# Stationary weights with a step of two, at eight places in turn

## The chip, the cores and the metric

The kernel runs on one core of one Trainium2 chip. The core has a matmul engine (PE; its weight loads are listed apart as PEld), a vector engine (DVE), a scalar engine (ACT), GpSimd (POOL) and a queue engine (SP) that issues the transfers. A matmul has two operands in the core's memory: a stationary one of 128 x 128 that is loaded into the array first, and a moving one whose columns are streamed through it; the result is added up in one of eight banks (128 x 512 words). The metric is the device time of one execution in microseconds. A profile of one execution gives the times of single instructions.

## What is computed

One layer of a decoder: 256 rows of 2048 channels, all float32. A combined input projection, two kinds of attention, an output projection, and a gated MLP with a causal convolution of width 3; each half is normalised and added to its input. Cut to its matrix products:

```python
h = rmsnorm(x, pre_mix_g[l])
proj = h @ w_in[l]                       # 2048 x 5392: q, k, v of two groups, forget gates
...
mix = jnp.concatenate([o_a, o_b], axis=-1) @ w_out[l]
x = x + rmsnorm(mix, post_mix_g[l])
h = rmsnorm(x, pre_ffn_g[l])
u = causal_dwconv(h @ w_up[l], conv_w[l], conv_b[l])      # 2048 x 11264
gate, val = jnp.split(u, 2, axis=-1)
y = (jax.nn.gelu(gate, approximate=True) * val) @ w_down[l]   # 5632 x 2048
x = x + rmsnorm(y, post_ffn_g[l])
```

## The kernel before

Every product of float32 numbers is made of three products of a shorter float format: each operand is split into a high part (rounded) and a low part (what is left), and high x high, high x low and low x high are added up. The weights pass through the core once. They come in units of 128 partitions x up to 1024 words (512 KB), by SP's queue, into five buffers `raw`. ACT makes the high part `whi` with a cast (L111, or L94 in `w_high`), DVE the low part `wlo` with a subtraction raw - whi (L114, or L97). There are five buffers of each part. The order on PE is that of the program; in some stretches the orders of ACT, DVE, POOL and SP are written out too.

Weights are used in two ways.

*Stationary weights* (`still=True`). In the input projection of queries and keys and in the whole up-projection the result is wanted with channels on the partitions. A unit holds 4 blocks of 128 rows of w (index `a`) and 256 channels, those of bank m = 0 and then those of bank m = 1, in each block. For each `a` and `m`, 128 x 128 weights are loaded, and the transposed activations `hT` stream past: 512 columns for a high part of the weights (256 of the activations' high part and 256 of their low part, L252), and 256 columns for a low part of the weights (L257). `proj_T` takes two units at a time: 14 matmuls of high parts, 16 of low parts, and the last 2 of high parts, the two banks by turns. With the pair before, runs of 16 and 16 arise. The very first projections go through `unit_T` (L220 high, L225 low), the first gate of the MLP through `first_gate` (L881 high, L877 low).

*Moving weights.* In the value projection, the output projection and the down projection (`mm3`, L275) the activations are stationary, and the weights are streamed.

Before the change a stationary block is read word after word: 128 words, 512 bytes. The high part lies at the start of its tile of 1024 words, the low part of stationary weights 80 words into its tile of 1152 words (`LOW`), the low part of moving weights at the start. `hT` and the high parts begin at multiples of 512 bytes.

After a projection ACT and DVE add a bank's two halves (L846, L847), POOL scales, and ACT and DVE do the convolution (L850 to L854), the gate (L918, L925) and the split of the result into G.

Of the kernel before, what the change touches and what calls it, by code (L numbers as in the profile page):

```python
# [8 lines left out]
F32 = mybir.dt.float32  # L9
F32R = mybir.dt.float32r  # L10
BF16 = mybir.dt.bfloat16
AF = mybir.ActivationFunctionType
ALU = mybir.AluOpType
# [4 lines left out]
P = 128  # L18
# [4 lines left out]
KT = D // P  # L23
# [7 lines left out]
def hybrid_layer(ctx: ExitStack, tc: tile.TileContext, x, pre_mix_g, w_in, b_forget, sinks,  # L31
# [3 lines left out]
    pe, act, dve, pool, sp = nc.tensor, nc.scalar, nc.vector, nc.gpsimd, nc.sync  # L35
# [6 lines left out]
    wp = ctx.enter_context(tc.tile_pool(name="wp", bufs=4))  # L42
# [20 lines left out]
    UNIT = 1024  # L63
    WB = 5
# [6 lines left out]
        return raw, a, c  # L71


    LOW = 80

    def w_parts(n, keep=None, still=False):


        if keep and keep[0] is None:
            return keep[1]  # L80
        if keep:
            return [keep[0].tile([P, UNIT], F32R, tag="h" + x, bufs=keep[1], name="w" + x)[:, :n]
                    for x in ("hi", "lo")]
        hi = wp.tile([P, UNIT], F32R, tag="whi", bufs=WB, name="whi")
        lo = wp.tile([P, UNIT + 128], F32R, tag="wlo", bufs=WB, name="wlo")
        c = LOW if still else 0
        return [hi[:, :n], lo[:, c:c + n]]

    def w_high(unit, keep=None, still=False):

        raw, a, c = unit
        n = a * c
        hi, lo = w_parts(n, keep, still)
        act.copy(hi, raw[:, :n])  # L94

        def low():
            dve.tensor_tensor(lo, raw[:, :n], hi.bitcast(F32), op=ALU.subtract)  # L97

        return [x.rearrange("p (a c) -> p a c", a=a) for x in (hi, lo)], low

    def w_split(unit, pin=False, keep=None, begun=None, between=None, still=False):

        raw, a, c = unit
        n = a * c
        hi, lo = begun or w_parts(n, keep, still)
        for i in range(2 if between else 1):
            cs = slice(i * 512, i * 512 + 512) if between else slice(0, n)
            if i:
                between()
            if not between or i:  # L110
                i1 = act.copy(hi[:, cs], raw[:, cs])  # L111
                if pin:
                    tc.keep_in_program_order(i1)
            i2 = dve.tensor_tensor(lo[:, cs], raw[:, cs], hi[:, cs].bitcast(F32), op=ALU.subtract)  # L114
            if pin:
                tc.keep_in_program_order(i2)
        return [x.rearrange("p (a c) -> p a c", a=a) for x in (hi, lo)]

    def w_unit(src, a, c, keep=None):
        return w_split(w_load(src, a, c), keep=keep)  # L120
# [21 lines left out]
    first = [[], []]  # L142
    head = wp.tile([P, UNIT], F32, tag="raw", bufs=5, name="raw")
    for i in range(2):
        cs = slice(i * 256, (i + 1) * 256)
# [39 lines left out]
    hT = main.tile([P, KT, 512], F32R, tag="hT", name="hT")  # L185
# [27 lines left out]
    def unit_T(parts, u, banks, ticks=True, halves=False):  # L213

        hi, lo = parts

        def high(a):
            kt = u * 4 + a
            for m, b in enumerate(banks):
                pe.matmul(b, hi[:, a, m * P:(m + 1) * P], hT[:, kt, :], start=(kt == 0),  # L220
                          stop=(kt == KT - 1))

        def low(a):
            for m, b in enumerate(banks):
                pe.matmul(b[:, 256:512], lo[:, a, m * P:(m + 1) * P],  # L225
                          hT[:, u * 4 + a, 0:256], start=False, stop=False)

        high(0)
        high(1)
        if halves:  # L230
            low(0)
            low(1)
        high(2)
        if ticks:
            tick()
        for a in range(2 if halves else 0, 4):
            low(a)
        high(3)
        if ticks:
            tick()  # L240

    def proj_T(w, c0, banks):

        for v in (0, 2):
            parts = [w_split(w_load(w_rows(w, u * 4, 4, c0, 256), 4, 256), still=True)
                     for u in (v, v + 1)]
            steps = [(u, a) for u in range(2) for a in range(4)]

            def high(u, a):
                kt = (v + u) * 4 + a  # L250
                for m, b in enumerate(banks):
                    pe.matmul(b, parts[u][0][:, a, m * P:(m + 1) * P], hT[:, kt, :],  # L252
                              start=(kt == 0), stop=(kt == KT - 1))

            def low(u, a):
                for m, b in enumerate(banks):
                    pe.matmul(b[:, 256:512], parts[u][1][:, a, m * P:(m + 1) * P],  # L257
                              hT[:, (v + u) * 4 + a, 0:256], start=False, stop=False)

            for n, (u, a) in enumerate(steps[:-1]):  # L260
                high(u, a)
                if n in (2, 5):
                    tick()
            for n, (u, a) in enumerate(steps):
                low(u, a)
                if n == 4:
                    tick()
            high(*steps[-1])
            tick()
# [11 lines left out]
    with tc.tile_pool(name="mixp", bufs=1) as mp:  # L281
# [47 lines left out]


        begun = w_parts(UNIT, still=True)
        tc.keep_in_program_order(dve.tensor_copy(begun[0][:, 0:512], head[:, 0:512]))
        x_part(0, (0,), "acc")
        bkv = [bank("att"), bank("att")]
        bq0 = [bank(), bank()]
        for u in range(4):
            if u:
                parts = w_split(first[0][u], True, still=True)
            else:
                parts = w_split(first[0][u], True, begun=begun,  # L340
                                between=lambda: x_part(0, (1,), "acc"))
            if u < 2:
                first_load(u + 2)
            unit_T(parts, u, bkv, False, u == 0)
            if u:
                x_square((2, 3, 2)[u - 1])
            parts = w_split(first[1][u], True, still=True)
            if u == 0:
                x_square(1)
            if u < 3:  # L350
                x_part(u + 1, (0, 1))
            else:
                for t in range(2):
                    st = small.tile([P, 1], F32, tag="st", name="st")
                    dve.tensor_reduce(st, sqx[t], axis=AX.X, op=ALU.add)
                    rpre.append(rstd_of(st, D, f"rpre{t}"))
                    dpre.append(diag_of(rpre[t]))
                later(2, rows_pre)
            unit_T(parts, u, bq0)
# [237 lines left out]
        for p0, npair, cols in ((0, 3, 384), (3, 3, 384), (6, 2, 272)):  # L597
# [3 lines left out]
            for k0 in range(0, KT, per):  # L601
                na = min(per, KT - k0)
                hi, lo = w_unit(w_rows(w_in, k0, na, c0, cols), na, cols)
                for a in range(na):
                    kt = k0 + a
# [104 lines left out]
        hT = hT2  # L710
# [55 lines left out]
        for n in (2, 3):  # L766
            for u in range(4):
                raw = w_load(w_rows(w_out, 8 + u * 2, 2, n * 512, 512), 2, 512)
# [43 lines left out]
    with tc.tile_pool(name="ffn", bufs=1) as fp:  # L812
# [45 lines left out]
        def first_gate():  # L858

            banks = [bank(), bank()]  # L860

            def one(t, u):
                ts = slice(t * P, t * P + P)

                both = u >= 2
                ls = slice(0, 256) if both else ts

                def v(x):
                    return x.rearrange("p (h t c) -> p h t c", h=2, t=2)[:, :, t, :]

                for low in (False, True)[:1 if both and t == 0 else 2]:
                    for kt in range(u * 4, u * 4 + 4):
                        hi, lo = gate[kt]
                        for m, b in enumerate(banks):
                            ms = slice(m * P, (m + 1) * P)
                            if low:
                                pe.matmul(b[:, 256 + ls.start:256 + ls.stop], lo[:, ms],  # L877
                                          hT[:, kt, ls], start=False,
                                          stop=(t == 1 and kt == KT - 1))
                            else:  # L880
                                pe.matmul(v(b), hi[:, ms], v(hT[:, kt, :]),  # L881
                                          start=(t == 0 and kt == 0), stop=False)

            one(0, 0)
            one(0, 1)
            one(0, 2)
            for high, low in [turn(1, u) for u in range(4)]:
                high()
                low()
            one(0, 3)  # L890
            lows[2]()
            x_squares(0)
            x_squares(1)
            rows = ffn_tables()
            for u in range(4):
                one(1, u)
            later(4, rows)
            return banks
# [3 lines left out]
        for half in range(2):  # L902
# [42 lines left out]
            for n in range(3 + (half == 0)):  # L945
                b2 = [bank(), bank()]
                for u in range(FHALF // 2):
                    hi, lo = w_unit(w_rows(w_down, half * FHALF + u * 2, 2, n * 512, 512), 2, 512)
# [33 lines left out]
        for u in range(FHALF // 2):  # L982
            hi, lo = w_unit(w_rows(w_down, FHALF + u * 2, 2, 1536, 512), 2, 512,
                            keep=(None, [rest[:, c:c + 2, :].rearrange("p a c -> p (a c)")
                                         for c in (4 * (u - LAST), 4 * (u - LAST) + 2)])
# [57 lines left out]
```

## Time and profile before

| | |
|---|---|
| median of 2 runs | 1080.03 us (1079.7 to 1080.36) |
| the profiled execution | 1079.4 us, span 1077.6 us |
| PE busy in the span | 1064.9 us, 99% |
| weight loads, busy | 926.9 us, 86% |
| DVE, ACT, POOL busy | 743.8, 619.4, 180.5 us |
| transferred | 202.88 MB, 188 GB/s in the mean |

The stretches of stationary weights lie at the start, in the attention part and in the up-projection (two halves); the moving weights' long stretches follow each half of the up-projection. Matmuls are pipelined, and their ends in the trace are modelled: a matmul's length there is longer than the time from its start to the next one's. The pace is therefore read from starts. The granted clock of PE is full nearly everywhere.

```profile
PE   9999999999999999999999999999999999999996
PEld 7899988887889888888888888888888888888886
DVE  5988878887568876777677444457777777765563
PEclk9999999999999999999999999999999999999999
```

Each digit is the busy share, in tenths, of a fortieth of the span.

### The profile page before, as it was taken

What the parts mean: (1) busy time and instruction counts of PE and PEld (TensorE: products, weight loads), DVE (VectorE), ACT (ScalarE), POOL (GpSimd) and SP (SyncE); (2) the same over time, 40 slices, a digit from 0 to 9 for tenths busy, and PEclk for the clock granted to TensorE, in tenths of its full rate; (3) what the DMA queues carried; (4) which work ended last, traced back from release to release, by engine and by line L of the source; (5) the groups of instructions that cost most, each with busy time, mean ns of one, the idle gap of its engine ahead of it and who ended that gap; (6) DMA issues with size and microseconds to landing.
All of it is one profiled execution on the core that took longest, in us unless ns stands there. A gap on an engine that the chain in (4) does not pass through costs nothing.

```text
span 1077.6 us, 16247 instructions
## 1 busy us (share of the span) xinstructions
PE 1064.9 (99%) x5986; PEld 926.9 (86%) x5986; DVE 743.8 (69%) x1200; ACT 619.4 (57%) x1060; POOL 180.5 (17%) x252
## 2 busy tenths in 40 slices
PE   9999999999999999999999999999999999999996
PEld 7899988887889888888888888888888888888886
DVE  5988878887568876777677444457777777765563
ACT  7766766667557755656565443456565555644450
POOL 3343244332022201101010000001010100101111
PEclk9999999999999999999999999999999999999999
DMA  8645556544863765555665666665556656565652
GB/s 294 209 120 172 176 171 207 159 149 156 300 227 112 235 193 192 194 189 186 194 193 180 200 197 191 195 192 190 186 192 193 193 182 195 188 198 193 193 166 78
DMA packets 164970, 202.88 MB, mean 188 GB/s; under 512 B 6780, under 2 KB 130972, under 8 KB 164380
## 3 DMA queue, kind: packets, MB, share of 16 engines
q1 hardware_dynamic: 164176, 201.27, 58.3%
q8 instruction: 47, 0.77, 0.3%
q10 hardware_dynamic: 716, 0.58, 0.2%
q14 instruction: 31, 0.25, 0.1%
HBM read 199.58 MB, written 2.11 MB: 187 GB/s over the span
## 4 chain that ended last, share of the span: by engine, by line
PE 89%; DVE 4%; ACT 2%; POOL 2%; issue 2%; DMA 2%; SPq 0%; POOLq 0%; DVEq 0%; ACTq 0%
PE bank_acc L275 34%; PE bank_acc L252 19%; PE bank_att L252 14%; PE bank_acc L257 10%; PE bank_att L257 7%; DVE wlo L114 2%; POOL scr L408 1%; PE bank_att L441 1%; PE bank_acc L881 1%; ACT p L459 1%; PE bank_att L476 1%; DMA x_in<-in_x_dram 1%; PE bank_acc L877 0%; ACT whi L111 0%; DMA c_dram<-scr 0%
## 5 line engine op out<-in xcount | busy, mean ns | idle before, releaser
L114 DVE TENSOR_TENSOR wlo<-raw,whi 128x1024 fp32r<-128x1024 f32 (+3 forms) x357 | 454.2, 1275 | 246.8 <-ACT whi L111 173.6
L111 ACT CAST whi<-raw 128x1024 fp32r<-128x1024 f32 (+3 forms) x356 | 367.9, 1035 | 182.2 <-PE bank_acc L275 117.4
L252 PE MATMUL bank_acc<-hT,whi 128*128 128x512 f32 x1088 | 266.9, 392 | 0.0
L252 PEld LDWEIGHTS bank_acc<-hT,whi 128*128 128x128 f32 x1088 | 198.2, 188 | 37.3
L275 PE MATMUL bank_acc<-whi,G 128*128 128x512 f32 (+1 forms) x724 | 214.5, 378 | 0.0
L275 PEld LDWEIGHTS bank_acc<-whi,G 128*128 128x128 f32 x724 | 133.8, 188 | 25.6
L252 PE MATMUL bank_att<-hT,whi 128*128 128x512 f32 x640 | 154.2, 391 | 0.0
L848 POOL TENSOR_TENSOR u<-u,rowf 128x256 f32<-128x256 f32 x88 | 55.5, 653 | 538.3 <-DVE u L847 536.0
L257 PEld LDWEIGHTS bank_acc<-hT,wlo 128*128 128x128 f32 x1088 | 138.3, 189 | 5.7
L257 PE MATMUL bank_acc<-hT,wlo 128*128 128x256 f32 x1088 | 141.8, 281 | 0.0
L252 PEld LDWEIGHTS bank_att<-hT,whi 128*128 128x128 f32 x640 | 117.6, 188 | 22.7
L275 PE MATMUL bank_acc<-wlo,G 128*128 128x512 f32 (+1 forms) x362 | 137.1, 379 | 0.0
L257 PEld LDWEIGHTS bank_att<-hT,wlo 128*128 128x128 f32 x640 | 81.0, 189 | 3.1
L275 PE MATMUL bank_acc<-whi,oT 128*128 128x512 f32 (+1 forms) x272 | 82.5, 380 | 0.0
L257 PE MATMUL bank_att<-hT,wlo 128*128 128x256 f32 x640 | 82.0, 281 | 0.0
L275 PEld LDWEIGHTS bank_acc<-wlo,G 128*128 128x128 f32 x362 | 68.1, 188 | 12.7
L275 PEld LDWEIGHTS bank_acc<-whi,oT 128*128 128x128 f32 x272 | 50.2, 188 | 9.3
L275 PE MATMUL bank_acc<-wlo,oT 128*128 128x512 f32 (+1 forms) x136 | 51.2, 377 | 0.0
L275 PE MATMUL bank_acc<-whi,hT 128*128 128x384 f32 (+1 forms) x192 | 47.5, 323 | 0.0
L846 ACT COPY cs<-bank_acc 128x256 f32<-128x256 f32 x48 | 15.9, 372 | 52.2 <-PE bank_acc L252 52.2
L459 ACT ACTIVATE p<-p,nm 128x256 f32<-128x256 f32 (+1 forms) x64 | 28.4, 445 | 26.9 <-DVE nm L447 26.9
L846 ACT COPY cs<-bank_att 128x256 f32<-128x256 f32 x40 | 13.3, 373 | 47.2 <-PE bank_att L252 47.2
(200 smaller groups left out, 1016.4 us busy)
## 6 DMA issues: line engine op xcount, KB each, us to landing
raw<-in_w_up_dram SPq DMA_DIRECT2D x176, 512.0 KB, 3.5
raw<-in_w_down_dram SPq DMA_DIRECT2D x88, 512.0 KB, 4.6
raw<-in_w_in_dram SPq DMA_DIRECT2D x51, 512.0 KB, 4.1
raw<-in_w_out_dram SPq DMA_DIRECT2D x32, 512.0 KB, 4.7
raw<-in_w_in_dram SPq DMA_DIRECT2D x16, 384.0 KB, 3.4
cb<-c_dram SPq DMA_DIRECT2D x8, 256.0 KB, 3.6
x_sb<-in_x_dram SPq DMA_DIRECT2D x2, 1024.0 KB
raw<-in_w_in_dram SPq DMA_DIRECT2D x5, 408.0 KB, 3.2
```

The costliest lines, as they stand in the source:

```text
L111: i1 = act.copy(hi[:, cs], raw[:, cs])
L114: i2 = dve.tensor_tensor(lo[:, cs], raw[:, cs], hi[:, cs].bitcast(F32), op=ALU.subtract)
L252: pe.matmul(b, parts[u][0][:, a, m * P:(m + 1) * P], hT[:, kt, :], start=(kt == 0), stop=(kt == KT - 1))
L257: pe.matmul(b[:, 256:512], parts[u][1][:, a, m * P:(m + 1) * P], hT[:, (v + u) * 4 + a, 0:256], start=False, stop=False)
L275: pe.matmul(b, a, r[:, cols], start=(first and i == 0), stop=(last and i == 2))
L408: pool.tensor_tensor(dst, dst, row, op=ALU.mult)
L441: pe.matmul(sb[e][:, cs], a[r, t * P:(t + 1) * P], b[r, 0:nk], start=(n == 0), stop=(n == 2))
L459: act.activation(p[:, e, cs], p[:, e, cs], AF.Exp, bias=nm[:, t, e:e + 1], scale=-1.0, accum_out=rs[:, t, e:e + 1])
L476: pe.transpose(pb[:, i * P:(i + 1) * P], p[:, e, c:c + P], ident)
L846: act.copy(c, b[:, 256:512])
L848: pool.tensor_tensor(u[:, 2:258], u[:, 2:258], rowf, op=ALU.mult)
L881: pe.matmul(v(b), hi[:, ms], v(hT[:, kt, :]), start=(t == 0 and kt == 0), stop=False)
```

## The change

In a tile of stationary weights the channels of the two banks now alternate word by word: the block of `a` holds channel 0 of bank 0, channel 0 of bank 1, channel 1 of bank 0, and so on. `w_views` gives the three views that the cast and the subtraction use: `raw` is read in the order in which it came, `hi` and `lo` are written (and `hi` read again) with a step of two words. A matmul takes `hi[:, a, m]`: 128 words with a step of two, out of 1024 bytes. The moving operand, the products and their order stay as they were.

The place of a part in its tile is no longer 0 for the high and 80 words for the low. It goes round eight places, 8 words (32 bytes) apart; two units that follow each other share a place; the low part goes round in another order than the high part, so that in time all pairs of places occur. Both tiles have 1088 words now (1024 and 1152 before), so the buffers of both parts, moving weights included, lie at another distance from each other. All else in memory stays where it was.

```diff
-    LOW = 80
+    still_no = [0]
...
-        hi = wp.tile([P, UNIT], F32R, tag="whi", bufs=WB, name="whi")
-        lo = wp.tile([P, UNIT + 128], F32R, tag="wlo", bufs=WB, name="wlo")
-        c = LOW if still else 0
-        return [hi[:, :n], lo[:, c:c + n]]
+        i = still_no[0] // 2
+        still_no[0] += still
+        cs = (i % 8 * 8, (i // 8 * 3 + i) % 8 * 8) if still else (0, 0)
+        return [wp.tile([P, UNIT + 64], F32R, tag="w" + x, bufs=WB, name="w" + x)[:, c:c + n]
+                for x, c in zip(("hi", "lo"), cs)]
+
+    def w_views(raw, hi, lo, a, still):
+
+        if still:
+            return (raw.rearrange("p (a m i) -> p a m i", a=a, m=2),
+                    *(x.rearrange("p (a i m) -> p a m i", a=a, m=2) for x in (hi, lo)))
+        return [x.rearrange("p (a c) -> p a c", a=a) for x in (raw, hi, lo)]
...
-        act.copy(hi, raw[:, :n])
+        raw, hi, lo = w_views(raw[:, :a * c], *w_parts(a * c, keep, still), a, still)
+        act.copy(hi, raw)
...
-                    pe.matmul(b, parts[u][0][:, a, m * P:(m + 1) * P], hT[:, kt, :],
-                              start=(kt == 0), stop=(kt == KT - 1))
+                    pe.matmul(b, parts[u][0][:, a, m], hT[:, kt, :], start=(kt == 0),
+                              stop=(kt == KT - 1))
...
-                    pe.matmul(b[:, 256:512], parts[u][1][:, a, m * P:(m + 1) * P],
+                    pe.matmul(b[:, 256:512], parts[u][1][:, a, m],
                               hT[:, (v + u) * 4 + a, 0:256], start=False, stop=False)
```

`w_split`, `unit_T` and `first_gate` are changed in the same way.

More of the change, by code (lines that the diff above doesn't have):

```diff
@@ L83, in w_parts @@
                     for x in ("hi", "lo")]
-        hi = wp.tile([P, UNIT], F32R, tag="whi", bufs=WB, name="whi")
-        lo = wp.tile([P, UNIT + 128], F32R, tag="wlo", bufs=WB, name="wlo")
-        c = LOW if still else 0
-        return [hi[:, :n], lo[:, c:c + n]]
+        i = still_no[0] // 2
[8 more added lines that the diff above has]
+        return [x.rearrange("p (a c) -> p a c", a=a) for x in (raw, hi, lo)]
     def w_high(unit, keep=None, still=False):
         raw, a, c = unit
-        n = a * c
-        hi, lo = w_parts(n, keep, still)
-        act.copy(hi, raw[:, :n])
+        raw, hi, lo = w_views(raw[:, :a * c], *w_parts(a * c, keep, still), a, still)
+        act.copy(hi, raw)
         def low():
-            dve.tensor_tensor(lo, raw[:, :n], hi.bitcast(F32), op=ALU.subtract)
-        return [x.rearrange("p (a c) -> p a c", a=a) for x in (hi, lo)], low
+            dve.tensor_tensor(lo, raw, hi.bitcast(F32), op=ALU.subtract)
+        return [hi, lo], low
     def w_split(unit, pin=False, keep=None, begun=None, between=None, still=False):
         raw, a, c = unit
-        n = a * c
-        hi, lo = begun or w_parts(n, keep, still)
+        raw, hi, lo = w_views(raw[:, :a * c], *(begun or w_parts(a * c, keep, still)), a, still)
         for i in range(2 if between else 1):
-            cs = slice(i * 512, i * 512 + 512) if between else slice(0, n)
+            r = slice(i * 2, i * 2 + 2) if between else slice(0, a)
             if i:
@@ L110, in w_split @@
             if not between or i:
-                i1 = act.copy(hi[:, cs], raw[:, cs])
+                i1 = act.copy(hi[:, r], raw[:, r])
                 if pin:
                     tc.keep_in_program_order(i1)
-            i2 = dve.tensor_tensor(lo[:, cs], raw[:, cs], hi[:, cs].bitcast(F32), op=ALU.subtract)
+            i2 = dve.tensor_tensor(lo[:, r], raw[:, r], hi[:, r].bitcast(F32), op=ALU.subtract)
             if pin:
                 tc.keep_in_program_order(i2)
-        return [x.rearrange("p (a c) -> p a c", a=a) for x in (hi, lo)]
+        return [hi, lo]
     def w_unit(src, a, c, keep=None):
@@ L219, in high @@
             for m, b in enumerate(banks):
-                pe.matmul(b, hi[:, a, m * P:(m + 1) * P], hT[:, kt, :], start=(kt == 0),
-                          stop=(kt == KT - 1))
+                pe.matmul(b, hi[:, a, m], hT[:, kt, :], start=(kt == 0), stop=(kt == KT - 1))
         def low(a):
             for m, b in enumerate(banks):
-                pe.matmul(b[:, 256:512], lo[:, a, m * P:(m + 1) * P],
-                          hT[:, u * 4 + a, 0:256], start=False, stop=False)
+                pe.matmul(b[:, 256:512], lo[:, a, m], hT[:, u * 4 + a, 0:256], start=False,
+                          stop=False)
         high(0)
@@ L331, in hybrid_layer @@
         begun = w_parts(UNIT, still=True)
-        tc.keep_in_program_order(dve.tensor_copy(begun[0][:, 0:512], head[:, 0:512]))
+        raw0, hi0, _ = w_views(head, *begun, 4, True)
+        tc.keep_in_program_order(dve.tensor_copy(hi0[:, 0:2], raw0[:, 0:2]))
         x_part(0, (0,), "acc")
@@ L339, in hybrid_layer @@
             else:
-                parts = w_split(first[0][u], True, begun=begun,
+                parts = w_split(first[0][u], True, still=True, begun=begun,
                                 between=lambda: x_part(0, (1,), "acc"))
@@ L874, in one @@
                         for m, b in enumerate(banks):
-                            ms = slice(m * P, (m + 1) * P)
                             if low:
-                                pe.matmul(b[:, 256 + ls.start:256 + ls.stop], lo[:, ms],
+                                pe.matmul(b[:, 256 + ls.start:256 + ls.stop], lo[:, m],
                                           hT[:, kt, ls], start=False,
@@ L880, in one @@
                             else:
-                                pe.matmul(v(b), hi[:, ms], v(hT[:, kt, :]),
+                                pe.matmul(v(b), hi[:, m], v(hT[:, kt, :]),
                                           start=(t == 0 and kt == 0), stop=False)
```

## The prediction

> **What bounds the kernel now.** I read the page first: the span, the busy row of the matmul engine and the chain that ended last.
>
> ```profile
> span 1077.6 us, 16247 instructions
> PE 1064.9 (99%) x5986; PEld 926.9 (86%) x5986; DVE 743.8 (69%) x1200; ACT 619.4 (57%) x1060; POOL 180.5 (17%) x252
> PE 89%; DVE 4%; ACT 2%; POOL 2%; issue 2%; DMA 2%; SPq 0%; POOLq 0%; DVEq 0%; ACTq 0%
> PE bank_acc L275 34%; PE bank_acc L252 19%; PE bank_att L252 14%; PE bank_acc L257 10%; PE bank_att L257 7%; DVE wlo L114 2%; POOL scr L408 1%; PE bank_att L441 1%; PE bank_acc L881 1%; ACT p L459 1%; PE bank_att L476 1%; DMA x_in<-in_x_dram 1%; PE bank_acc L877 0%; ACT whi L111 0%; DMA c_dram<-scr 0%
> ```
>
> The matmul queue never rests, and half of the chain (19 + 14 + 10 + 7 = 50%) lies in the lines that the change touches, L252 and L257. A busy PE can still be a waiting PE, so the waits come next. These are all that PE has:
>
> ```profile
> PE bank_acc L168 <- DVE junk L163: 1.3, 1, 1.3
> PE bank_att L441 <- ACT keys L278: 0.9, 1, 0.9
> PE bank_att L441 <- DVE keys L279: 0.8, 1, 0.8
> PE bank_acc L300 <- DMA x_in<-in_x_dram: 0.6, 1, 0.6
> PE bank_att L300 <- DMA x_in<-in_x_dram: 0.2, 1, 0.2
> ```
>
> 3.8 us in all, none of it in L252 or L257. So nothing feeds PE too late; what counts is the pace at which one matmul follows another. That pace is read from the timeline of the up-projection (start, length, line, count): from the start of one run to the start of the next, divided by the count.
>
> ```profile
> 504.83 2.05 PE L257 MATMUL bank_att<-hT,wlo 128*128 128x256 f32 x16
> 506.72 3.81 PE L252 MATMUL bank_att<-hT,whi 128*128 128x512 f32 x16
> 510.37 2.05 PE L257 MATMUL bank_att<-hT,wlo 128*128 128x256 f32 x16
> ```
>
> A high part (512 columns): (510.37 - 506.72)/16 = 228.1 ns. A low part (256 columns): (506.72 - 504.83)/16 = 118.1 ns. What would they cost if they only streamed columns? Two places with stationary operands at round addresses give it, the down projection and the first gate:
>
> ```profile
> 600.17 0.62 PE L275 MATMUL bank_acc<-whi,G 128*128 128x512 f32 x2
> 600.62 0.39 PE L275 MATMUL bank_acc<-wlo,G 128*128 128x512 f32 x1
> 600.85 0.62 PE L275 MATMUL bank_acc<-whi,G 128*128 128x512 f32 x2
> ...
> 336.40 1.12 PE L881 MATMUL bank_acc<-hT,whi 128*128 128x256 f32 x8
> 337.36 1.00 PE L877 MATMUL bank_acc<-hT,wlo 128*128 128x128 f32 x8
> ...
> 341.05 1.91 PE L728 MATMUL bank_att<-ident,x_sb 128*128 128x128 f32 x16
> ...
> L728 PE MATMUL bank_att<-ident,x_sb 128*128 128x128 f32 x32 | 4.0, 272 | 0.0
> ```
>
> 512 columns: 0.68/3 = 226.7 ns; 256 columns: 0.96/8 = 120.0 ns. The difference is 106.7 ns for 256 columns, 0.417 ns a column, and 120.0 - 106.7 = **13.3 ns of every matmul are not columns**. The transposes (L728) stream 128 columns, 53 ns, and still need (1.91 - 0.27)/15 = 109.3 ns each: there the load of 128 weights is what takes the time. 109.3 ns are 262 column times, which fits two for each weight and 6 (2.5 ns) for the change of weights. So of the 13.3 ns some 2.5 look unavoidable, and 10.8 look like two readers in each other's way: while a matmul streams, the next weights are read beside it. One thing in the rows says that addresses matter: L257's low parts lie 80 words into their tile, and go at 118.1 ns where L881's, as wide and at place 0, go at 120.0.
>
> [...]
>
> **The change, part by part.** No instruction is added, removed or moved: the same casts, subtractions, loads and matmuls in the same order, with other addresses.
>
> 1. *Stationary reads with a step of two.* These groups get them:
>
> ```profile
> L252 PE MATMUL bank_acc<-hT,whi 128*128 128x512 f32 x1088 | 266.9, 392 | 0.0
> L252 PE MATMUL bank_att<-hT,whi 128*128 128x512 f32 x640 | 154.2, 391 | 0.0
> L257 PE MATMUL bank_acc<-hT,wlo 128*128 128x256 f32 x1088 | 141.8, 281 | 0.0
> L257 PE MATMUL bank_att<-hT,wlo 128*128 128x256 f32 x640 | 82.0, 281 | 0.0
> L220 PE MATMUL bank_att<-hT,whi 128*128 128x512 f32 x32 | 9.0, 398 | 0.1
> L225 PE MATMUL bank_att<-hT,wlo 128*128 128x256 f32 x32 | 4.7, 284 | 0.0
> L881 PE MATMUL bank_acc<-hT,whi 128*128 128x256 f32 x64 | 9.1, 287 | 0.0
> ```
>
> 1728 highs and 1728 lows (108 times 3.65 + 1.89 us = 598 us), 64 and 64 in the first projections (each row again for the other banks), 64 and 48 in the first gate. Today the two readers walk at different speeds: a weight takes two column times, so the weights advance 4 bytes while the moving columns advance 8. The faster walks past the slower again and again, and meets it wherever the two need the same part of the memory. With a step of two the weights also advance 8 bytes in two column times. Two readers at equal speed either never meet, or meet once, one waits, and they are apart from then on. I take this reading, since it is the one by which a place can count at all. Bounds: the gain can't exceed what leaves the streams alone. High: 228.1 - (213.3 + 2.5) = 12.3 ns, times 1728 = 21.3 us. Low: 118.1 - 109.3 (the load's own time) = 8.8 ns, times 1728 = 15.2 us. The 240 others: about 2 us. Together 38.5 us. I take nine tenths, 34.7 us, because some of the eight places must start with a meeting.
>
> 2. *Strided writes by ACT and DVE, strided reads by DVE.* These are the rows of a stretch of up-projection, with the busy shares of that stretch (PE, PEld, DVE, ACT, POOL, clock, DMA share, GB/s):
>
> ```profile
> L114 DVE TENSOR_TENSOR wlo<-raw,whi 128x1024 fp32r<-128x1024 f32 x36 | 47.2, 1312 | 24.4 <-ACT whi L111 9.1 <-issue 6.1 <-PE bank_acc L257 5.5
> L111 ACT CAST whi<-raw 128x1024 fp32r<-128x1024 f32 x37 | 38.8, 1048 | 10.0 <-PE bank_acc L252 5.8 <-PE bank_att L252 4.2
> 400.00:500.00 100.00, 100.00 (x581) 88.38 (x579) 72.94 (x107) 59.24 (x91) 11.18 (x18) 1.00 0.59 190
> ```
>
> I cost them at nothing. The cover is DVE's idle 27.1 us of 100: 36 subtractions may grow by 0.75 us each, from 1.31 to 2.06, before DVE and not PE sets the pace. No row of this trace has an ACT or DVE operand with a step, so from below it is nothing and from above a doubling (rival 2). [...]
>
> 3. *Other places for the moving weights.* The tiles' pitch changes, so every other buffer of L275's moving operand shifts by half of 512 bytes against its stationary one.
>
> ```profile
> L275 PE MATMUL bank_acc<-whi,G 128*128 128x512 f32 (+1 forms) x724 | 214.5, 378 | 0.0
> L275 PE MATMUL bank_acc<-wlo,G 128*128 128x512 f32 (+1 forms) x362 | 137.1, 379 | 0.0
> ```
>
> A place was worth 1.9 ns above (120.0 against 118.1); half of these 1086 by 1.9 ns is 1 us, either way. I take 0.
>
> With PE faster by 6% there, DVE goes from 73% to 78% of its time, ACT from 59% to 63%, DMA from 0.59 to 0.63. Nothing new comes late.
>
> **Sum.** The profiled execution took 1079.4 us (span 1077.6), 0.6 below the median of the two runs, 1080.03. 1079.4 - 34.7 = 1044.7; on the median's footing 1045.
>
> **The rivals.**
>
> 1. *Every line that the weights touch costs the moving stream a turn.* Then a step of two touches twice as many, and the 10.8 ns double: 10.8 x 3696 matmuls = 40 us, 1120. For it: the rows of two widths can't tell a cost of each load from one of each meeting. Against it: the place of the low parts changes the cost, which a cost of each line would not.
> 2. *Strided operands slow DVE.* It decides from 2.06 us a subtraction. Doubled, DVE would need 25.7 + 36 x 2.62 = 120 us for 100, and the 598 us grow by 20%: 1199; with 2.3 us, 108 for 100, 1127. [...]
> 3. *The weights load more slowly with a step.* At half speed 218.6 ns for 128: the highs still hide it (228.1), the lows cannot: 100.5 ns x 1840 and 6 us more for L881, 1270. Slower than before it is from a load of about 130 ns on, where what the lows lose equals the highs' 12.3 ns. Against it: the moving stream reads 9.6 bytes a ns already, and stepped weights would ask for no more lines a ns than that.
> 4. *The 13.3 ns are a fixed cost of a matmul,* or only some places profit: 1058 to 1080.
>
> **Chances.** The forecast 0.53 (1039 to 1057 by itself: all 38.5 us and 2 us for place at one end, 60% of the gain at the other); rival 4 0.12; rival 1 0.13; rival 2 0.12; rival 3 0.10. Two per cent, 22 us, is about what a measurement can tell from no change here: below 1058.4 lies the forecast (0.53), within lies rival 4 (0.12), above 1101.6 lie the other three (0.35). The range takes in the forecast, rival 4 and rival 1: 1038 to 1122, 0.78, and the mildest of rival 2.
>
> **What would show it.** In the timeline of the up-projection, sixteen highs should take 3.45 to 3.5 us from start to start and sixteen lows 1.75 to 1.8; 3.8 and 2.06 speak for rival 1, and 3.65 and 1.89 for rival 4. The subtraction of 1024 columns should stay near 1.3 us and the cast near 1.05; over 2.06, with PE waiting for DVE in the list of waits, is rival 2. The weight loads' mean of 188 ns, and lows above 200 ns with highs unchanged, are rival 3. The down projection should keep 226.7 ns. The forecast is wrong if the paces of the eight places scatter so much that bad ones eat the gain.

## The result, and the profile after

The changed kernel takes 1091.91 us (median of 2 runs, 1091.88 to 1091.93) against 1080.03: **1.1% slower**, ratio 1.011 with a 95% interval of 1.0093 to 1.0126. By the 2% bound of the prediction that is no change; its sign and its size are clear all the same, and the sign is the other one than forecast.

The page of the changed kernel, the lines that answer to those shown of before (L252 is now L259, L257 is L264, L275 is L282, L111 is L119, L114 is L122):

```profile
span 1090.0 us, 16247 instructions
PE 1078.9 (99%) x5986; PEld 946.5 (87%) x5986; DVE 737.4 (68%) x1200; ACT 637.6 (58%) x1060; POOL 184.3 (17%) x252
PE 93%; DVE 2%; ACT 1%; DMA 1%; POOL 1%; issue 1%; SPq 0%; DVEq 0%; POOLq 0%; ACTq 0%
L259 PE MATMUL bank_acc<-hT,whi 128*128 128x512 f32 x1088 | 271.7, 396 | 0.0
L282 PE MATMUL bank_acc<-whi,G 128*128 128x512 f32 (+1 forms) x724 | 214.6, 378 | 0.0
L264 PE MATMUL bank_acc<-hT,wlo 128*128 128x256 f32 x1088 | 144.7, 284 | 0.0
L259 PEld LDWEIGHTS bank_acc<-hT,whi 128*128 128x128 f32 x1088 | 205.5, 195 | 34.6
L264 PEld LDWEIGHTS bank_acc<-hT,wlo 128*128 128x128 f32 x1088 | 142.0, 196 | 5.6
```

PE's busy time grew by 14.0 us and the span by 12.4. The down projection (L282) kept its 378 ns, the matmuls of stationary weights and their loads (188 and 189 ns before) grew. All of PE's waits, again:

```profile
PE bank_acc L176 <- DVE junk L171: 1.3, 1, 1.3
PE bank_att L449 <- ACT keys L285: 0.7, 1, 0.7
PE bank_acc L307 <- DMA x_in<-in_x_dram: 0.4, 1, 0.4
```

No new wait. So PE is not fed later, it goes more slowly, and the timeline of the same stretch of up-projection says where:

```profile
507.06 3.91 PE L259 MATMUL bank_att<-hT,whi 128*128 128x512 f32 x16
510.80 2.08 PE L264 MATMUL bank_att<-hT,wlo 128*128 128x256 f32 x16
512.72 3.89 PE L259 MATMUL bank_att<-hT,whi 128*128 128x512 f32 x16
516.45 2.09 PE L264 MATMUL bank_att<-hT,wlo 128*128 128x256 f32 x16
```

Sixteen highs take 3.74 and 3.73 us (3.65 before), sixteen lows 1.92 (1.89): a high 233.4 ns instead of 228.1, a low 120.0 instead of 118.1. For 108 such runs that is 108 x (0.085 + 0.03) = 12.4 us, the whole difference. Two runs hit it that closely by luck: in the mean of the 94 undisturbed runs (see the next section) a run grew by 0.111 us, highs by 4.6 ns and lows by 2.3, and 108 x 0.111 = 12.0 us. The other engines, in a stretch of the same length (casts and subtractions first, then the busy shares in the order PE, PEld, DVE, ACT, POOL):

```profile
L119 ACT CAST whi<-raw 128x1024 fp32r<-128x1024 f32 x36 | 40.8, 1134 | 10.1 <-PE bank_acc L259 5.8 <-PE bank_att L259 4.3
L122 DVE TENSOR_TENSOR wlo<-raw,whi 128x1024 fp32r<-128x1024 f32 x36 | 46.5, 1292 | 26.6 <-ACT whi L119 10.7 <-issue 6.9 <-PE bank_acc L264 5.3
400.00:500.00 100.00, 100.00 (x565) 89.21 (x564) 70.90 (x106) 61.84 (x90) 11.14 (x18) 1.00 0.60 186
```

The subtraction with a step costs what it did (1292 ns, 1312 before), the cast 8% more (1134, 1048 before). Neither is late.

### The profile page after: what moved, and what is told of

Its sections match the earlier page's. It is cut to its first block, busy times and chain, and to the rows that moved or that the text cites. A ratio compares the mean times of both kernels' runs of the same rounds, so it can differ in the third digit from the quotient of the medians.

```text
span 1090.0 us, 16247 instructions
## 1 busy us (share of the span) xinstructions
PE 1078.9 (99%) x5986; PEld 946.5 (87%) x5986; DVE 737.4 (68%) x1200; ACT 637.6 (58%) x1060; POOL 184.3 (17%) x252
## 4 chain that ended last, share of the span: by engine, by line
PE 93%; DVE 2%; ACT 1%; DMA 1%; POOL 1%; issue 1%; SPq 0%; DVEq 0%; POOLq 0%; ACTq 0%
PE bank_acc L282 34%; PE bank_acc L259 21%; PE bank_att L259 14%; PE bank_acc L264 11%; PE bank_att L264 7%; PE bank_att L449 1%; PE bank_att L484 1%; PE bank_acc L888 1%; DVE wlo L122 1%; PE bank_att L508 1%; PE bank_acc L884 1%; ACT whi L119 0%; PE bank_att L228 0%; DMA c_dram<-scr 0%; DMA x_in<-in_x_dram 0%
## 5 line engine op out<-in xcount | busy, mean ns | idle before, releaser
L122 DVE TENSOR_TENSOR wlo<-raw,whi 128x1024 fp32r<-128x1024 f32 (+3 forms) x357 | 449.7, 1262 | 263.3 <-ACT whi L119 182.6
L119 ACT CAST whi<-raw 128x1024 fp32r<-128x1024 f32 (+3 forms) x356 | 387.5, 1091 | 183.9 <-PE bank_acc L282 120.8
L259 PE MATMUL bank_acc<-hT,whi 128*128 128x512 f32 x1088 | 271.7, 396 | 0.0
L259 PEld LDWEIGHTS bank_acc<-hT,whi 128*128 128x128 f32 x1088 | 205.5, 195 | 34.6
L282 PE MATMUL bank_acc<-whi,G 128*128 128x512 f32 (+1 forms) x724 | 214.6, 378 | 0.0
L259 PE MATMUL bank_att<-hT,whi 128*128 128x512 f32 x640 | 157.1, 395 | 0.0
L282 PEld LDWEIGHTS bank_acc<-whi,G 128*128 128x128 f32 x724 | 133.7, 188 | 25.6
L264 PEld LDWEIGHTS bank_acc<-hT,wlo 128*128 128x128 f32 x1088 | 142.0, 196 | 5.6
L264 PE MATMUL bank_acc<-hT,wlo 128*128 128x256 f32 x1088 | 144.7, 284 | 0.0
L259 PEld LDWEIGHTS bank_att<-hT,whi 128*128 128x128 f32 x640 | 121.9, 195 | 21.1
L282 PE MATMUL bank_acc<-wlo,G 128*128 128x512 f32 (+1 forms) x362 | 137.1, 379 | 0.0
L264 PEld LDWEIGHTS bank_att<-hT,wlo 128*128 128x128 f32 x640 | 83.0, 196 | 3.0
L264 PE MATMUL bank_att<-hT,wlo 128*128 128x256 f32 x640 | 83.5, 283 | 0.0
L282 PE MATMUL bank_acc<-whi,oT 128*128 128x512 f32 (+1 forms) x272 | 82.4, 380 | 0.0
L282 PEld LDWEIGHTS bank_acc<-wlo,G 128*128 128x128 f32 x362 | 68.1, 188 | 12.7
L282 PEld LDWEIGHTS bank_acc<-whi,oT 128*128 128x128 f32 x272 | 50.2, 188 | 9.3
L282 PE MATMUL bank_acc<-wlo,oT 128*128 128x512 f32 (+1 forms) x136 | 51.2, 377 | 0.0
L282 PE MATMUL bank_acc<-whi,hT 128*128 128x384 f32 (+1 forms) x192 | 47.5, 323 | 0.0
```

The lines of the kernel that those rows point to most:

```text
L119: i1 = act.copy(hi[:, r], raw[:, r])
L122: i2 = dve.tensor_tensor(lo[:, r], raw[:, r], hi[:, r].bitcast(F32), op=ALU.subtract)
L259: pe.matmul(b, parts[u][0][:, a, m], hT[:, kt, :], start=(kt == 0), stop=(kt == KT - 1))
L264: pe.matmul(b[:, 256:512], parts[u][1][:, a, m], hT[:, (v + u) * 4 + a, 0:256], start=False, stop=False)
L282: pe.matmul(b, a, r[:, cols], start=(first and i == 0), stop=(last and i == 2))
```

## The experiments

In what follows a "run" is one of 16 highs and 16 lows on PE. Its length, and the pace of single matmuls, come from the starts of the matmuls in the trace; a pace is also given as **column times over**: divided by 0.417 ns, less the 512 or 256 columns. 32 column times are the 13.3 ns of the prediction, 6 are its 2.5 ns. Means of runs are over the 94 runs in which nothing stands between the 32 matmuls. Each ratio is against runs of the kernel before that were timed beside that kernel (medians of 1080.03 to 1080.54 us).

| kernel | run, us | time, us | ratio to before, 95% |
|---|---|---|---|
| before | 5.54 | 1080.03 | |
| the change | 5.65 | 1091.91 | 1.0093 to 1.0126 |
| step of two, places of before | 5.65 | 1091.84 | 1.0089 to 1.0119 |
| no step, eight places | 5.60 | 1086.53 | 1.0041 to 1.0071 |
| no step, sixteen places | 5.60 | 1086.56 | 1.0039 to 1.0072 |
| step of four, places of before | 7.52 | 1322.22 | 1.222 to 1.2257 |
| no step, 48 and 48 words | 5.52 | 1078.56 | 0.9975 to 0.9993 |
| no step, 0 and 60 words | 5.53 | 1079.47 | 0.9981 to 0.9999 |
| before, all 64 bytes on | 5.54 | 1080.85 | 0.9994 to 1.0011 |
| step of two, 16 and 0 words | 5.61 | 1087.78 | 1.0058 to 1.0086 |
| no step, columns in one line | 5.28 | 1054.06 | 0.9723 to 0.978 |
| step of two, columns in one line | 5.38 | 1065.61 | 0.983 to 0.9887 |
| no step, columns back to front | 5.62 | 1088.35 | 1.005 to 1.0095 |
| step of two, columns back to front | 5.62 | 1088.48 | 1.0054 to 1.0099 |
| step of two, 64 places | 5.64 | 1089.64 | 1.0058 to 1.0117 |
| no step, sixteen places, back to front | 5.64 | 1089.55 | 1.0057 to 1.0116 |
| step of two, sixteen places, back to front | 5.64 | 1089.76 | 1.0059 to 1.0118 |

**The two halves of the change apart.** First the step alone. `place` gives the offsets of the high and the low part in words.

```diff
-        cs = (i % 8 * 8, (i // 8 * 3 + i) % 8 * 8) if still else (0, 0)
+        cs = (0, 80) if still else (0, 0)
```

(and the tiles' sizes of before, 1024 and 1152 words)

> The step of two alone, with the places and tile sizes of before (high part at 0, low part 80 words in). Before, a run of 16 highs and 16 lows took 3.65 + 1.89 = 5.54 us; with the whole change it takes some 5.65. Theory L (each further line that the weights touch costs the columns about half a column time, wherever it lies): highs near 233 ns, lows near 120 ns, 5.65 us a run, 1090 to 1093 us. Theory P (the step is harmless, the loss comes from the eight places): 5.54 us a run or less, 1080 us. Theory M (two readers at equal speed, which can meet for good at a bad place): far from 5.65 either way, by 0.1 us or more, since one place is kept.

The timeline of this kernel:

```profile
506.85 3.89 PE L268 MATMUL bank_att<-hT,whi 128*128 128x512 f32 x16
510.57 2.08 PE L273 MATMUL bank_att<-hT,wlo 128*128 128x256 f32 x16
512.50 3.89 PE L268 MATMUL bank_att<-hT,whi 128*128 128x512 f32 x16
```

3.72 and 1.93 us: the step alone costs all of it, 1091.84 us. L had the paces and the time; P falls, and M with it. Then the places alone, the weights again word after word (the change's kernel with a step of one):

> The eight places in turn and the tile sizes of the change, but the weights read word after word, as before. Theory L: highs 227 ns, lows a little over before's because the good place of 80 words is lost (118 to 120 ns): 5.55 to 5.57 us a run, 1080 to 1084 us. Theory P: the whole loss is here, 5.65 us a run, 1092 us. Theory M says the same as L here.

```profile
508.43 2.05 PE L273 MATMUL bank_att<-hT,wlo 128*128 128x256 f32 x16
510.32 3.84 PE L268 MATMUL bank_att<-hT,whi 128*128 128x512 f32 x16
514.01 2.08 PE L273 MATMUL bank_att<-hT,wlo 128*128 128x256 f32 x16
515.93 3.88 PE L268 MATMUL bank_att<-hT,whi 128*128 128x512 f32 x16
```

3.69 and 1.89 or 1.92: the places alone cost half, 6 us: more than L and M allowed, less than P. So either half of the change loses, and the two losses do not add: 11.4 and 6.1 us apart, 11.9 together, as if both took away in part the same thing.

**Which places.** Sixteen places 16 bytes apart, word after word:

```diff
+        return i % 16 * 4, (i // 16 * 5 + i) % 16 * 4
```

> Weights read word after word, high and low parts each at sixteen places 16 bytes apart in turn (all pairs of places within the first 256 of them), to read the pace of each place in one execution. Theory L (place hardly counts for highs): highs 226 to 228 ns at every place, lows 117 to 120, 1080 to 1084 us. Theory M (meetings of two readers): the pace depends on the place with a period, some places of the highs well under 226 ns, as the lows' 80 words are under the place 0 by 2 ns.

Column times over for a high, by the offset of its weights in bytes (mean of the fourth to thirteenth high of each run, the top twentieth left out):

| 0 | 16 | 32 | 48 | 64 | 80 | 96 | 112 | 128 | 144 | 160 | 176 | 192 | 208 | 224 | 240 |
|---|---|---|---|---|---|---|---|---|---|---|---|---|---|---|---|
| 32.4 | 48.0 | 47.7 | 47.7 | 47.6 | 44.4 | 50.1 | 47.9 | 46.3 | 44.5 | 47.2 | 38.3 | 36.8 | 44.7 | 47.7 | 33.6 |

**The place at which the high parts lay before, 0, is the best of sixteen; most others cost 48.** Lows range from 19 (64 bytes) to 32. With the step of two, over the change's eight places: 47.9, 44.5, 39.2, 47.8, 42.4, 48.0, 47.8, 48.5. The step puts the highs where the worse places put them anyway: over all sixteen places word after word the mean is 44, over these eight with the step 46. L falls here. By it a cost comes with each line that the weights touch. I counted 16 bytes as a line, which is my assumption and is shown by no run: then 128 words lie in 32 lines word after word and in 64 with the step of two, and 32 lines cost as much as 64 at most places (47.2 to 50.1 at eight of the sixteen, 47.8 to 48.5 at five of the eight). M had only the half of it: the pace does depend on the place, but no place lies under 226 ns. In the changed kernel the two units of a pair lie, in four pairs of five, an odd multiple of 256 bytes apart, and go alike (highs 40.0 and 39.5 at 64 bytes, 47.7 and 48.0 at 96): by that the places repeat after 256 bytes. Is it the address that counts, or the place against the columns? The kernel before, with everything behind a small pool 64 bytes further on, columns and weights alike:

```diff
-    const.tile([P, 120], F32, tag="room", name="room_c")
+    const.tile([P, 136], F32, tag="room", name="room_c")
```

> The kernel before with everything behind the first pool, columns and weights alike, 64 bytes further on. High parts that lay 64 bytes away from their columns' start went at 233 ns where those at 0 went at 227. If what counts is the place of the weights against the columns: nothing changes, 226.7 and 118 ns, 1080 us. If it is the address itself: highs near 233 ns, 1088 us.

```profile
507.38 3.82 PE L252 MATMUL bank_att<-hT,whi 128*128 128x512 f32 x16
511.03 2.05 PE L257 MATMUL bank_att<-hT,wlo 128*128 128x256 f32 x16
512.92 3.82 PE L252 MATMUL bank_att<-hT,whi 128*128 128x512 f32 x16
```

3.65 and 1.89, as before to the digit, though weights 64 bytes from their columns' start cost 47.6: the place against the columns counts.

**Is it two readers at all?** In the next pair `proj_T` streams the first four words of each column block again and again, so that the moving reader stays in one line; its products aren't the layer's.

```diff
+    def one_line(x):
+        return x[:, 0:4].unsqueeze(1).to_broadcast([P, x.shape[1] // 4, 4])
...
-                    pe.matmul(b, parts[u][0][:, a, m * P:(m + 1) * P], hT[:, kt, :],
+                    pe.matmul(b, parts[u][0][:, a, m * P:(m + 1) * P], one_line(hT[:, kt, :]),
```

> The kernel before, but in the queries', keys' and up-projections the matmuls stream the same four words of the columns again and again (as many columns as before; so the products aren't the layer's): the moving reader stays in one line of 16 bytes. If the 13.3 ns that a matmul takes beyond its columns come from two readers meeting in the memory: they shrink towards 2.5 ns, highs 216 to 220, lows 110 to 114 ns, 5.2 to 5.35 us a run of 16 and 16. If they are a fixed cost of a matmul, or come from the weights' lines alone: 5.54 us as before.

> The same four words streamed, with the weights read with a step of two (places of before). Readers that meet: 5.2 to 5.35 us a run as in the run beside it, so that the step's 0.11 us a run are gone. A cost of each line that the weights touch: 5.65 us, the step's 0.11 us stay. A mixture would show as a rest of the 0.11.

The timelines, first word after word, then with the step of two:

```profile
511.33 1.95 PE L260 MATMUL bank_acc<-hT,wlo 128*128 128x256 f32 x16
513.12 3.64 PE L255 MATMUL bank_acc<-hT,whi 128*128 128x512 f32 x16
516.60 1.95 PE L260 MATMUL bank_acc<-hT,wlo 128*128 128x256 f32 x16
```

```profile
506.52 2.04 PE L276 MATMUL bank_att<-hT,wlo 128*128 128x256 f32 x16
508.39 3.65 PE L271 MATMUL bank_att<-hT,whi 128*128 128x512 f32 x16
511.88 2.04 PE L276 MATMUL bank_att<-hT,wlo 128*128 128x256 f32 x16
```

Highs go at 217.5 and 218.1 ns, and from the fourth to the thirteenth high of a run they have 9 column times over in both: **what highs lose beyond these, with or without the step, they lose only when the columns are read along the memory.** Together with the places, which count only against the columns, that speaks for two readers. That the other pattern of the columns plays no part by itself is not shown.

The run as a whole says something else. It takes 5.28 us as the first expectation had it, but 5.38 with the step, outside the 5.2 to 5.35 of readers that meet: 0.10 of the step's 0.11 us a run stay, and 11.6 us of time. They only change places. With columns read along the memory the step costs a high 4.5 ns and a low 2.2 in the mean (5.54 to 5.65 us a run), in one line it costs a high 0.7 and a low 5.5. So lows go at 111.9 and 116.9 ns here, and by estimate this is the load's own time: it is over the low's stream (106.7 ns), and the load with a step is 6 ns longer:

```profile
L276 PEld LDWEIGHTS bank_acc<-hT,wlo 128*128 128x128 f32 x1088 | 140.2, 197 | 3.4
```

(191 ns in the kernel beside it.)

**More lines still.** A step of four: the channels of two blocks and two banks by turns.

```diff
+            b = 2 * a // STEP
+            return (raw.rearrange("p (b q i) -> p b q i", b=b, q=STEP),
+                    *(x.rearrange("p (b i q) -> p b q i", b=b, q=STEP) for x in (hi, lo)))
```

> A step of four words: the channels of two blocks and two banks by turns, each weight in a line of 16 bytes of its own; places and tile sizes of before. Theory L, line for line: highs lose twice what the step of two cost on top of it (64 further lines where that added 32), 16 to 32 column times more, near 245 ns, lows near 130 ns: about 6.0 us a run, 1125 to 1145 us. Theory P: 1080 us. Theory M (the weights now walk twice as fast as the columns, so the readers pass each other again): about before's 5.5 us a run if the load keeps its pace. All three leave out that ACT and DVE, with a step of 16 bytes, may become slower: over 2.06 us a subtraction PE would wait for them, and then the paces inside a run are to be read, not the time.

```profile
504.60 3.78 PE L273 MATMUL bank_att<-hT,wlo 128*128 128x256 f32 x16
508.22 4.04 PE L268 MATMUL bank_att<-hT,whi 128*128 128x512 f32 x16
512.10 3.78 PE L273 MATMUL bank_att<-hT,wlo 128*128 128x256 f32 x16
...
L273 PEld LDWEIGHTS bank_acc<-hT,wlo 128*128 128x128 f32 x1088 | 260.4, 327 | 0.5
...
L131 DVE TENSOR_TENSOR wlo<-raw,whi 128x1024 fp32r<-128x1024 f32 x24 | 49.4, 2065 | 17.6 <-ACT whi L128 12.8 <-PE bank_acc L273 3.1 <-PE bank_att L273 1.8
```

All theories missed: the load itself breaks down, 327 ns instead of 189 for lows and 313 instead of 188 for highs, a low takes 226 ns (118), and the subtraction 2065 ns instead of 1312. That is the prediction's third rival, but at a step of four words. The highs' 242.5 ns are those of a whole run, and by the lows' 226 ns a load now takes, by estimate, nearly as long as they do. From the fourth to the thirteenth high they have 52 column times over, where the step of two at the same place has 48; L asked for 16 to 32 more.

**Can a place rescue the step?** First the pair with the shortest run in the changed kernel's own profile, kept throughout:

> The step of two at one pair of the change's eight places, the one with the shortest run in its own profile: high part 16 words in, low part at 0 (5.60 us a run there, 5.65 in the mean). If a good place can rescue the step: 5.54 us or less, 1080 us. If the step costs its 15 column times nearly wherever the weights lie: 5.58 to 5.65 us, 1085 to 1092 us.

1087.78 us: no. Then all 64 places one word apart in turn (`i * 13 % 64` for the high part):

> The step of two at all 64 places one word apart in turn. If equal speed helps at the right place: some places of the highs at 6 to 20 column times over the 512 (216 to 222 ns). If equal speed is no help: highs at 36 to 50 at all places, 1086 to 1093 us.

1089.64 us; a high has 40 to 51 column times over, place by place (two neighbours taken together), 44 in the mean, and the lowest mean of a single run is 39.8. Word after word it was 32 at place 0, and also 44 in the mean of sixteen places: equal speed is no help to highs, and no harm either, but for the best places.

**Or the other direction?** In the prediction's picture equal speed helps only readers that walk the same way; which way the weights are read, no trace shows. So the columns were turned round in `proj_T` (the results' columns lie the other way round):

```diff
-                    pe.matmul(b, parts[u][0][:, a, m * P:(m + 1) * P], hT[:, kt, :],
+                    pe.matmul(b, parts[u][0][:, a, m * P:(m + 1) * P], hT[:, kt, ::-1],
```

> The kernel before, but in proj_T the columns are streamed from the last to the first (so the result's columns lie the other way round); the weights word after word. My prediction took it that weights and columns walk the same way. If instead the weights are read from their last word, the two walk towards each other, 12 bytes per two column times, and meet 6 times in a load (1536 bytes, by the 256 bytes after which the places repeat); with the columns turned round they walk the same way, 4 bytes apart, and meet twice. Theory B (read from the back): overhead 10 to 20 column times instead of 32, highs 217 to 222 ns, 5.25 to 5.45 us a run. Theory F (read from the front, as predicted): now they walk against each other and meet oftener: highs over 230 ns, 5.6 us or more. A cost per line touched: 5.54 us, no change.

> The step of two with the columns streamed from the last to the first. Theory B: now the two walk the same way at the same speed, what the prediction had in mind: highs 216 to 222 ns, lows near 110, 5.2 to 5.4 us a run, some 1045 to 1060 us. Theory F: they walk against each other at 16 bytes per two column times, highs over 235 ns, 5.7 us or more. A cost per line touched: 5.65 us, as with the columns forward.

Both 48 column times over for highs, 1088.35 and 1088.48 us. One place says little, so both at sixteen:

> Columns from the last to the first, weights word after word, at sixteen places 16 bytes apart in turn. At one place the highs had 48 column times over, as at most places with the columns forward. If direction counts: another spread over the places than with the columns forward (32 to 50), some well under 30. If not: the same spread with its good place shifted.

> The same with the step of two. If the weights are read from the back, weights and columns now walk the same way at the same speed: at most places hardly a meeting, 6 to 20 column times over, and at a few a bad one. If direction is no help: 36 to 50 everywhere, as forward.

The timeline of the last:

```profile
505.94 3.90 PE L268 MATMUL bank_att<-hT,whi 128*128 128x512 f32 x16
509.67 2.05 PE L273 MATMUL bank_att<-hT,wlo 128*128 128x256 f32 x16
511.56 3.90 PE L268 MATMUL bank_att<-hT,whi 128*128 128x512 f32 x16
```

3.73 us. Word after word the highs have 47.6 to 55.7 over at the sixteen places, with the step 47.5 to 55.7 (1089.55 and 1089.76 us). In this direction the step changes nothing for highs, nor for lows (117.8 ns with and without it at the first place), and neither theory of the direction holds: B missed both of its kernels, F was right only of the first, and at sixteen places the good ones are gone instead of shifted. No place lies under 47.5.

**A version that beats both.** From the runs over the places, word after word:

> Word after word, but one place kept: high and low parts both 48 words (192 bytes) into their tiles, a pair that was among the shortest in the runs over the places (a run of 16 highs and 16 lows took 5.48 us there, 5.54 before). Theory M2 (the cost is two readers meeting, set by the place of the weights against the columns and by the phase in which a run begins): 5.46 to 5.52 us a run, 1072 to 1078 us. Theory L2 (a cost per line touched, places are noise): 5.54 to 5.60 us, 1080 to 1087 us.

> Word after word, the high part at 0 as before, the low part 60 words (240 bytes) in instead of 80: 5.51 us a run in the run over the places. Theory M2: highs 226.7 ns as before, lows 116 to 117 instead of 118, 1076 to 1079 us. Theory L2: 1080 us.

48 and 48 words is the faster, 1078.56 us, 0.16% under before (0.07 to 0.25%), 0 and 60 words 0.1% (0.01 to 0.19%); both less than hoped. The timeline of 48 and 48 words shows why:

```profile
438.93 1.98 PE L273 MATMUL bank_acc<-hT,wlo 128*128 128x256 f32 x16
440.74 3.82 PE L268 MATMUL bank_acc<-hT,whi 128*128 128x512 f32 x16
444.40 2.05 PE L273 MATMUL bank_acc<-hT,wlo 128*128 128x256 f32 x16
446.28 3.84 PE L268 MATMUL bank_acc<-hT,whi 128*128 128x512 f32 x16
449.96 1.98 PE L273 MATMUL bank_acc<-hT,wlo 128*128 128x256 f32 x16
```

The sixteen lows take 1.81 and 1.88 us by turns, at the same places: they fall into a good rhythm (some 16 column times over) or a bad one (some 26). A projection has two such runs; in the first half of the up-projection the second of them has the good rhythm, in the second half the first. So it is neither the place nor the run's part of the work. That it depends on where the run before left off would fit, and was not tested.

## Why the prediction was wrong

*That PE's pace is the bound, and not a wait,* was right: the difference lies in the 108 runs (12.0 us in the mean), none in the list of waits.

*That 10.8 of the 13.3 ns are two readers in each other's way* was right for most of it: with the columns in one line 9 column times are left of the 32 to 34 that the highs had, so 23 to 25 (some 10 ns) go when the columns' reader stays in one line. The 2.5 ns that the bounds took as unavoidable were an estimate from the transposes' 109.3; the least that a run showed for highs is these 9 column times, 3.8 ns.

*The step that failed* is the one on which the 34.7 us rested: "Two readers at equal speed either never meet, or meet once, one waits, and they are apart from then on." With the step of two, highs have 40 to 51 column times over at all 64 places, and 47.5 to 55.7 with the columns turned round. In its place the runs show a cost of 38 to 51 column times at nearly all places, of either speed, often near 48 and 44 in the mean over the places with the step as without it; that is no smaller with the columns turned round (47.5 to 55.7), and falls to 32 to 37 only for weights read word after word at three of sixteen places. The kernel before had its highs at the best of these (32), and I read its 13.3 ns as the price of a collision that could be avoided; it was already the good case. The change takes the highs from 228.1 to 233.4 ns, 1728 x 5.3 ns = 9.2 us (4.6 ns and 7.9 us in the mean of the runs), where the prediction had them gain up to 21.3. The sign of the forecast turned on that: the rows had two places only, 0 for all highs and 80 words for all lows, and I took the small difference between them for the whole reach of the place. The sign of being wrong that I had named, bad places that eat the gain, is not what came: even the best of the change's eight places (39) is slower than the kernel before.

*The low's bound* was mis-sized: I let a low fall to the load's own 109.3 ns. With the step the load is 7 ns longer (196 against 189), and a low with the columns out of the way takes 116.9 ns, so at most 1.2 of the 8.8 ns, 2 of the 15.2 us, were there to gain. With the columns in its way it takes 120.0 (118.1 before): 1728 x 1.9 ns = 3.3 us, the rest of the 12.4 (2.3 ns and 4.0 us in the mean). The same longer load touches the sentence before the one that failed, that stepped weights go as fast as the columns: if the 111.9 and 116.9 ns of the one-line pair are the load's, stepped weights lag by an estimated 4 to 5%, and no run tells equal speed that fails to help from a speed that was never quite equal.

*ACT and DVE at nothing* was right as far as PE goes, which waits for neither: a step of two words costs DVE nothing (1292 ns, 1312 before), ACT 8% (1134, 1048 before), the load 4% (196, 189 before); a step of four costs DVE 57% (2065 ns) and the load of the lows 73% (327 ns).

*Other places for the moving weights at 0* was right: L282 has 214.6 us, 214.5 before.

*The rivals.* The first had the sign, a third of the size (12 us of 40), and not the mechanism: at most places 32 lines (of 16 bytes, as I counted them) cost the 48 column times that 64 do, and 128 cost 52. The second did not come: no run shows the 2.3 us or the doubled 2.62 that it took for a subtraction, and the step of two gave 1292 ns. The third came in part, 7 ns a load (196 against 189). The range held the time only because it reached to the first rival; by the 2% bound the result is the "no change" to which I gave 0.12, and it came another way than I had named.

*Open* is why the cost so often lies near 48, why place 0 with words in sequence escapes it, and why readers at one speed, or nearly so, do not. That readers at one speed lock into a rhythm in which they keep meeting would fit, but no run here shows it.

## What to carry to other kernels

Before a layout is changed to save a small cost of each matmul, find out with one kernel that goes round the places whether the present one is an average or already a good case: one profile holds the pace of every place. A matmul engine that is 99% busy and waits for nothing can still lose some 5% of a stretch, which came back here when the moving operand stayed in one line (5.54 us a run against 5.28), and start-to-start times divided by the count are where it shows. A step of two words in 4-byte data cost DVE nothing (1292 ns, 1312 without), ACT 8% (1134, 1048) and the weight load 4% (196, 189); one of four cost DVE 57% (2065) and the load of the lows 73% (327).

## What was not expected of the hardware

- The pace of a matmul depends on the place of the stationary operand against the moving one: word after word 32 to 50 column times over the 512 for highs, 19 to 32 over the 256 for lows, and no change when both move by 64 bytes together (3.65 and 1.89 us for sixteen of each, as before).
- At the same places a stream of matmuls can go in two rhythms: lows at 113 or 118 ns, by turns from run to run, with high and low parts 48 words into their tiles.
- With the moving operand in one line of 16 bytes, the kernel as a whole takes 1054 us, 2.5% less. By estimate this is about all that a layout of the stationary weights could bring to these projections; no run shows one that comes near it.
- A stationary operand with a step of four words loads in 313 (highs) and 327 ns (lows) instead of 188 and 189, and a kernel that is otherwise the same takes 22% longer.
